# The last third of a feed-forward down projection: six plain accumulations against seven block products

## The chip, the cores and the metric

The kernel runs on one core of a Trainium2 chip. The time is the device time of one execution in microseconds (us); lower is better. The engines are named as the profile names them: PE is the matrix engine, PEld its weight load, DVE the vector engine, ACT the scalar engine, POOL the general engine that also issues DMAs, SP the engine that only issues DMAs.

## The reference, cut to what matters

The model is a two-layer decoder trunk on 512 tokens of width 1024 in float32. Each layer ends in a gated feed-forward block with 2816 hidden columns, and the change lies in its last matrix product, `@ w_down`.

```python
def swiglu(h, w_gate, w_up, w_down):
    return (jax.nn.silu(h @ w_gate) * (h @ w_up)) @ w_down
...
for i in range(DEPTH):                       # DEPTH = 2
    ...
    x = x + swiglu(rmsnorm(x, ffn_norm[i]), w_gate[i], w_up[i], w_down[i])
    if i == N_A_LAYERS - 1:                  # after layer 0
        kv = (rmsnorm(x, kv_norm) @ w_kv_shared)
return rmsnorm(x, final_norm)
```

After layer 0 the next work needs two normalised copies of `x` (for `b_in` and for `w_kv_shared`). After layer 1 only the final norm and the store of the output follow.

## The kernel before

**Three matmuls for one.** Every float32 operand is split into a high part (ACT copies it into a rounded type, `hi_of`, L153) and a low part (DVE subtracts, `lo_of`, L156). A product is three matmuls: high with high, high with low, low with high (`three`). Weights come by DMA into `raw` tiles (two buffers) and are split into `wh` and `wl` tiles (nine buffers with the tag "w", shared by high and low parts). The nine buffers let the splitting run about four weight pieces ahead of PE; a new piece waits until PE has done with an old one.

**The feed-forward block.** `ffn` (L797) takes the 2816 hidden columns in steps `c` of 256, eleven of them, in the groups of `FF_GROUPS`: steps 0 to 3, 4 to 7 and 8 to 10. In a step it makes gate and up (tiles `g` and `u`) for two tiles of 128 hidden columns, with all 512 tokens, and their product `sg`. After each group the group's part of the down projection is added onto the residual, the four tiles `xt[0]` to `xt[3]` (128 tokens by 1024 columns each, printed as `x`).

**Two ways for the down projection.** The first two groups (`SEVEN`) are done by `seven_products` (L713): tokens, hidden columns and output columns are halved, and the 2 by 2 block product, eight block products as it stands, is made from seven products of sums of blocks (Strassen's scheme in Winograd's form). `seven_lhs` makes the sums on the side of the hidden values, once for each step: `e`, `o`, `d` (128x512) and `n` (128x256), each split in high and low. The sums on the side of the weights are made by DMAs that add onto a tile in place (`accum_op=ALU.add`, issued by POOL) and by DVE adds (`plus`). The third group is done plainly, by `by_token` (L393): for each half of the 1024 output columns, for each of the four token tiles, the products over six tiles of hidden columns are summed in one bank (`d`), and `residual` adds the bank to `x`.

**What follows the third group.** For each token tile, when its second half is in, ACT makes the sum of squares (`square_sum`), DVE the mean (`ms`), POOL the power -1/2 (`rstd`), and `then` is called. In layer 0 that is `both_norms` (L862): `Normed.add` scales the tile to `xn_hmix`, and once two tiles are there, generators (`turn`) transpose them on PE and split them into `hmix1` and `hkv`. PE goes on with `first.run` (tiles `pb`): four products of 24 matmuls of 256 columns for tokens 0 to 255, then the same for tokens 256 to 511. In layer 1 `gained` multiplies `x` by the final gain, `finish` scales by `rstd` and SP stores the result.

**Order.** Each engine runs its instructions in the order in which a scheduler wrote them; `keep` and `keep_in_program_order` hold chosen ones in the order of the code.

Of the kernel before, what the change touches and what calls it, by code (L numbers as in the profile page):

```python
# [16 lines left out]
P = 128  # L17
# [23 lines left out]

SEVEN = FF_GROUPS[:2]
# [64 lines left out]
def trunk(ctx: ExitStack, tc: tile.TileContext, x, mem, mix_norm, a_in, conv_w, b_in,  # L107
# [38 lines left out]
    ordered = [True]  # L146

# [8 lines left out]
    def lo_of(dst, src, hi):  # L156
        keep(nc.vector.tensor_tensor(dst, src, hi.bitcast(F32), ALU.subtract))  # L157
# [111 lines left out]
    def rstd_of(ss, name):  # L269
        m = small.tile([P, 1], F32, tag="ms", name=f"ms_{name}")  # L270
        keep(nc.vector.tensor_scalar(m, ss[:, 0:1], ss[:, 1:2], EPS, ALU.add, ALU.add))
# [101 lines left out]
    class Opening:  # L373
# [5 lines left out]

        def prepare(self):  # L380
            self.gets = self.first() + self.second()
            self.w = [get() for get in self.gets[:2]]
# [107 lines left out]
    def zero_rows(kl):  # L490

        for hh in range(2):
            nc.gpsimd.memset(kl[HD - hh * HD:P - hh * HD, hh, :].bitcast(F32), 0.0)
# [205 lines left out]
    def seven_lhs(even, odd, name):  # L699

        h0, h1 = slice(0, 256), slice(256, 512)
# [14 lines left out]
        def at(operand, hl, t):  # L716
            y, hf = home[operand]
            return y[:, hl, hf * 256 + t * P:hf * 256 + (t + 1) * P]
# [3 lines left out]
    def seven_products(w, g0, lhs, name):  # L722

        n = len(lhs)
        rows4 = w[2 * g0 * P:2 * (g0 + n) * P, :].rearrange("(c two p) n -> p c two n", two=2, p=P)

        def block(i, j):
            return rows4[:, :, i, j * 512:(j + 1) * 512]

        def load(raw, first, second=None):  # L730
            tc.keep_in_program_order(nc.sync.dma_start(raw, block(*first)))
            if second is not None:
                tc.keep_in_program_order(nc.gpsimd.dma_start(raw, block(*second), accum_op=ALU.add))
            return raw

        def product(make, operand, raw):
            banks = [make(f"{operand}_{name}{t}") for t in range(2)]
            for c in range(0, n, 2):
                wp = split(raw[:, c:c + 2, :], 2, 512)
                for j in range(2):  # L740
                    for t in range(2):
                        three(banks[t], lambda hl: lhs[c + j](operand, hl, t), lambda hl: wp[hl][:, j, :],
                              c + j == 0, c + j == n - 1)
                        lanes.pump()
            return banks

        def copies(banks):
            held = [t2([P, S], F32, f"v_{name}{t}") for t in range(2)]
# [4 lines left out]
        def plus(dst, raw):  # L753
            for c in range(0, n, 2):
                nc.vector.tensor_tensor(dst[:, c:c + 2, :], dst[:, c:c + 2, :], raw[:, c:c + 2, :], ALU.add)

        def onto(t, hf, v, op=ALU.add):
            part = xt[t][:, hf * 512:(hf + 1) * 512]
            nc.vector.tensor_tensor(part, part, v, op)

        shape = [P, n, 512]
# [3 lines left out]
        v = copies(product(acc, "A11", r1))  # L765
        for t in range(2):
            onto(t, 0, v[t])
        u = copies(product(acc, "N1", r2))
# [28 lines left out]
    def ffn(layer, h, chains, opening, then, half=lambda t, hf: None):  # L797
        ss = sums(f"ssf{layer}")
        pending = []
        for g0, g1 in FF_GROUPS:  # L800
            hid = {}
            seven = (g0, g1) in SEVEN
            for c in range(g0, g1):
# [5 lines left out]
                for i in range(2):  # L809
# [14 lines left out]
                    if not seven:  # L824
                        hid[f] = split_y(sg, f"hid{layer}{f}")
                    elif i == 0:
                        even = sg
                    else:
                        hid[c] = seven_lhs(even, sg, f"hid{layer}{c}")
            if seven:  # L830
                pending += seven_products(w_down[layer], g0, [hid[c] for c in range(g0, g1)], f"d{layer}{g0}")
                continue
            last = g1 == 11
            for hf in range(2):
                def done(t, b):
                    residual(t, hf, b, ss if last else None, f"f{layer}{g0}")
                    if last:
                        half(t, hf)
                    if last and hf == 1:
                        then(t, rstd_of(ss[t], f"f{layer}{t}"))  # L840
                by_token(w_down[layer], [[2 * c, 2 * c + 1] for c in range(g0, g1)], hf * 512, 512,
                         ylhs(lambda k: hid[k]), NT, f"d{layer}{g0}{hf}", done, tail=TAIL if last and hf else 1)
# [19 lines left out]
    def both_norms(t, r):  # L862
        nq.add(t, xt[t], r)
        if t == 1:
            first.prepare()

    first = Opening(lambda i: acc(f"pb{i}"), lambda: cols(b_in[0], MAIN), lambda: cols(b_in[0], 0))
    ffn(0, h, nh.chains, opening, both_norms)
# [6 lines left out]
    for kl in key_lo:  # L875
        zero_rows(kl)
# [134 lines left out]
    def gained(t, hf):  # L1011
        if hf == 0:
# [11 lines left out]
    ffn(1, h, nh.chains, opening, finish, gained)  # L1024
# [26 lines left out]
```

## Time and profile before

| | |
|---|---|
| three runs, us | 1144.94, 1145.65, 1145.78 (median 1145.65) |
| profiled execution, us | 1145.12 |
| its span, first to last instruction, us | 1143.4 |
| mean granted clock of PE | 0.998 of full speed |
| PE busy, share of the span | 99% |
| DVE, ACT, POOL busy | 61%, 46%, 7% |
| third group of layer 0, first matmul to last | 524.45 to 558.85 us |
| third group of layer 1, first matmul to last | 1103.96 to 1136.6 us |

A row of the timeline gives the start in us from the start of the span, the time in us, engine, line, operation, "output<-inputs", and in brackets how long the engine stood idle before it and what ended that. A line of the kernel can be that of a helper. Rows of the chain of waits are start, length and what; rows of the groups give busy time, mean ns of one and idle time before. Where instructions of one engine follow each other closely their spans overlap, so what one costs there is the distance between starts.

### The profile page before, as it was taken

The page shows a single profiled execution, that of the slowest core. Times are in us where ns is not written, and L with a number is a line of the kernel's source. Part 1 is how long each engine was busy: PE and PEld are TensorE (multiplying, and loading weights), DVE is VectorE, ACT ScalarE, POOL GpSimd, SP SyncE. Part 2 cuts the span into 40 slices and gives each one's busy share as a digit, 9 for nine tenths or more (in the row PEclk, how much of TensorE's full clock was granted, in tenths as well). Part 3 has the DMA queues.
Part 4 walks back from the last instruction along what each step waited for, and adds up shares of the span by engine and source line. Part 5 has one row for each costly group of instructions (what it writes and reads, how often), then busy time and mean ns, then how long its engine had stood idle before and what let it go on. Part 6 is the DMA issues. An engine that isn't in the chain of part 4 may idle for free.

```text
span 1143.4 us, 14862 instructions
## 1 busy us (share of the span) xinstructions
PE 1130.9 (99%) x5844; PEld 963.2 (84%) x5844; DVE 699.5 (61%) x1044; ACT 524.1 (46%) x896; POOL 76.3 (7%) x155
## 2 busy tenths in 40 slices
PE   9999999999999999999999999999999999999997
PEld 9898888988888888888988988788888888888886
DVE  5767453553774468434678799986546844485335
ACT  7555423533432344233666677665434332353223
POOL 1100000000000001000100123321000000000000
PEclk9999999999999999999999999999999999999999
DMA  8332422247332742414222211122274244542311
GB/s 259 111 111 74 144 78 74 74 142 190 111 111 74 219 108 79 141 62 130 75 74 75 74 56 56 38 75 92 74 220 123 66 143 149 109 148 76 126 57 74
DMA packets 97456, 122.10 MB, mean 107 GB/s; under 512 B 2217, under 2 KB 73963, under 8 KB 97387
## 3 DMA queue, kind: packets, MB, share of 16 engines
q1 hardware_dynamic: 93040, 112.73, 30.1%
q0 software_dynamic: 4224, 8.39, 4.3%
q8 instruction: 46, 0.75, 0.3%
q14 instruction: 23, 0.19, 0.1%
q10 hardware_dynamic: 123, 0.03, 0.0%
HBM read 119.05 MB, written 2.10 MB: 106 GB/s over the span
## 4 chain that ended last, share of the span: by engine, by line
PE 92%; issue 3%; DVE 2%; ACT 1%; POOL 1%; DMA 1%; POOLq 0%; ACTq 0%; SPq 0%; DVEq 0%
PE u L136 22%; PE g L136 19%; PE A_d L136 6%; PE d L136 5%; PE o L136 5%; PE N_d L136 4%; PE S_d L136 4%; PE gu L136 4%; PE bg L136 3%; PE v L136 3%; PE k L136 2%; PE pa L136 2%; PE cg L136 2%; PE q L136 1%; PE pb L136 1%
## 5 line engine op out<-in xcount | busy, mean ns | idle before, releaser
L157 DVE TENSOR_TENSOR wl<-raw,wh 128x1024 fp32r<-128x1024 f32 x180 | 220.0, 1222 | 281.3 <-PE u L136 136.5
L154 ACT ACTIVATE wh<-raw 128x1024 fp32r<-128x1024 f32 x180 | 191.0, 1061 | 264.6 <-PE u L136 75.8
L819 ACT ACTIVATE sg<-g 128x512 f32<-128x512 f32 x40 | 23.9, 598 | 105.5 <-PE g L136 105.5
L136 PE MATMUL g<-hffn0h,wh 128*128 128x512 f32 x160 | 62.3, 389 | 0.0
L136 PE MATMUL g<-hffn0l,wh 128*128 128x512 f32 x160 | 62.3, 389 | 0.0
L136 PE MATMUL g<-hffn1h,wh 128*128 128x512 f32 x160 | 62.3, 389 | 0.0
L136 PE MATMUL g<-hffn1l,wh 128*128 128x512 f32 x160 | 62.3, 389 | 0.0
L136 PE MATMUL g<-hffn0h,wl 128*128 128x512 f32 x160 | 62.2, 389 | 0.0
L136 PE MATMUL u<-hffn0h,wh 128*128 128x512 f32 x160 | 62.2, 389 | 0.0
L136 PE MATMUL u<-hffn0l,wh 128*128 128x512 f32 x160 | 62.2, 389 | 0.0
L136 PE MATMUL u<-hffn0h,wl 128*128 128x512 f32 x160 | 62.2, 389 | 0.0
L136 PE MATMUL g<-hffn1h,wl 128*128 128x512 f32 x160 | 62.2, 389 | 0.0
L136 PE MATMUL u<-hffn1h,wh 128*128 128x512 f32 x160 | 62.2, 389 | 0.0
L136 PE MATMUL u<-hffn1l,wh 128*128 128x512 f32 x160 | 62.2, 389 | 0.0
L136 PE MATMUL u<-hffn1h,wl 128*128 128x512 f32 x160 | 62.2, 389 | 0.0
L136 PE MATMUL d<-wh,hid 128*128 128x512 f32 x192 | 59.7, 389 | 0.0
L154 ACT ACTIVATE wh<-b_d 128x1024 fp32r<-128x1024 f32 x32 | 33.7, 1060 | 34.2 <-PE u L136 15.3
L920 DVE TENSOR_TENSOR_SCAN sn<-sn 128x127 f32<-128x127 f32 (+3 forms) x48 | 40.3, 840 | 4.8 <-POOL sn L901 4.4
L136 PEld LDWEIGHTS d<-wh,hid 128*128 128x128 f32 x192 | 36.0, 188 | 7.5
L157 DVE TENSOR_TENSOR wl<-b_d,wh 128x1024 fp32r<-128x1024 f32 x32 | 38.9, 1221 | 4.1 <-PE N_d L136 2.3
L136 PE MATMUL d<-wl,hid 128*128 128x512 f32 x96 | 37.4, 389 | 0.0
L136 PEld LDWEIGHTS u<-hffn0l,wh 128*128 128x128 f32 x160 | 30.0, 188 | 6.3
(777 smaller groups left out, 2937.9 us busy)
## 6 DMA issues: line engine op xcount, KB each, us to landing
raw<-in_w_gate_dram SPq DMA_DIRECT2D x22, 1024.0 KB, 5.3
raw<-in_w_up_dram SPq DMA_DIRECT2D x22, 1024.0 KB, 5.4
raw<-in_w_down_dram SPq DMA_DIRECT2D x12, 1024.0 KB, 6.6
raw<-in_a_in_dram SPq DMA_DIRECT2D x8, 1024.0 KB, 5.5
b_d<-in_w_down_dram SPq DMA_DIRECT2D x8, 1024.0 KB, 7.5
raw<-in_w_o_dram SPq DMA_DIRECT2D x12, 512.0 KB, 3.6
raw<-in_w_kv_shared_dram SPq DMA_DIRECT2D x6, 1024.0 KB, 5.0
raw<-in_w_mem_kv_dram SPq DMA_DIRECT2D x4, 1024.0 KB, 5.2
```

Of the source, the lines that this page charges most:

```text
L136: nc.tensor.matmul(dst, a, b, start=start, stop=stop)
L154: keep(nc.scalar.activation(dst, src, AF.Copy))
L157: keep(nc.vector.tensor_tensor(dst, src, hi.bitcast(F32), ALU.subtract))
L819: nc.scalar.activation(sg, bg, AF.Silu)
L920: nc.vector.tensor_tensor_scan(back, back, back, 1.0, ALU.mult, ALU.bypass)
```

## The change

The third group of each layer is made by seven block products too, in a function of its own, `last_products`. Their order is S3, S2, A11, N1, A22, A12, N4. The halves of the tokens are exchanged in `seven_lhs` for that group, so that tokens 0 to 255 are complete after the fifth product (A22) and tokens 256 to 511 after the seventh (N4). The weight sums T3 and T2 are loaded ahead by one SP load each with one and two accumulating DMAs; T1 and T4 are then made in the same tiles in two pieces (`change`), T1 by SP loads with accumulating POOL DMAs behind them, T4 by accumulating POOL DMAs; the block B22 is loaded into T1's tile. Ten times in a layer, a result that goes into a second place of `x` is added there by a POOL DMA from a copy (`dma_onto`). The loads and splits of the next stage's first weights (`first` in layer 0) are called at fixed places within the group, and `zero_rows` (memsets of `kl`) is held in program order behind it.

```diff
-SEVEN = FF_GROUPS[:2]
...
-    def seven_lhs(even, odd, name):
-
-        h0, h1 = slice(0, 256), slice(256, 512)
+    def seven_lhs(even, odd, last, name):
+
+        h0, h1 = (slice(256 * (i ^ last), 256 * (i ^ last) + 256) for i in range(2))
...
+    def dma_onto(t, hf, v):
+        tc.keep_in_program_order(nc.gpsimd.dma_start(x_part(t, hf), v, accum_op=ALU.add))
...
+    def last_products(w, g0, lhs, name, ss, half, then, opening):
...
+        r2 = load(big_tile(shape, F32, f"t3_{name}"), (0, 1), (1, 1))
+        r1 = load(big_tile(shape, F32, f"t2_{name}"), (0, 0), (0, 1), (1, 1))
+        r3 = load(raw_tile(shape), (0, 0))
+        r4 = load(raw_tile(shape), (1, 0))
+        b3 = product(att, "S3", s.pieces(r2))
+        s.change(r2, (0, 0), (0, 1), anew=True)
+        b2 = product(acc, "S2", s.pieces(r1))
+        s.change(r1, (1, 0))
+        p, _ = parts(r3)
+        if opening is not None:
+            opening.load()
+        v = s.copies(b2, "v")
+        d = [t2([P, S], F32, f"d_{name}{t}") for t in range(2)]
+        for t in range(2):
+            dma_onto(2 + t, 1, v[t])
+            nc.vector.tensor_tensor(d[t], b3[t], v[t], ALU.subtract)
+            onto(t, 1, d[t], ALU.subtract)
+        b1 = product(acc, "A11", p)
+        p, _ = parts(r2)
+        s.change(r2, (1, 1), anew=True)
+        for t in range(2):
+            onto(t, 0, b1[t])
+            onto(t, 1, b1[t], ALU.subtract)
+            dma_onto(t, 0, d[t])
+            both = slot([P, 2, S], F32, f"a11_{name}{t}")
+            for i, sign in enumerate((1.0, -1.0)):
+                nc.scalar.activation(both[:, i, :], b1[t], AF.Copy, scale=sign)
+                dma_onto(2 + t, i, both[:, i, :])
+        bu = product(acc, "N1", p)
+        p, _ = parts(r1)
+        u = s.copies(bu, "u")
+        for t in range(2):
+            onto(t, 1, bu[t])
+            squares(t, 1)
+            half(t, 1)
+            dma_onto(2 + t, 1, u[t])
...
+        p12, before = parts(r4)
+        product(att, "A22", p, c21)
+        if opening is not None:
+            opening.load()
+            opening.split()
+        for t in range(2):
+            then(t, rstd_of(ss[t], f"{name}{t}"))
+        p, before = parts(r2)
+        if opening is not None:
+            opening.split()
+        for t, b in enumerate(product(att, "A12", p12)):
+            with tc.issue_after(before.ins):
+                onto(2 + t, 0, b)
+            squares(2 + t, 0)
+            half(2 + t, 0)
...
+        def c12(t, b):
+            with tc.issue_after(last_ms[0].ins):
+                onto(2 + t, 1, b)
+            squares(2 + t, 1)
+            half(2 + t, 1)
+            then(2 + t, rstd_of(ss[2 + t], f"{name}{2 + t}"))
+
+        product(acc, "N4", p, c12)
...
-                    if not seven:
-                        hid[f] = split_y(sg, f"hid{layer}{f}")
...
-            last = g1 == 11
-            for hf in range(2):
-                def done(t, b):
-                    residual(t, hf, b, ss if last else None, f"f{layer}{g0}")
...
+            if not last:
+                pending += seven_products(w_down[layer], g0, lhs, f"d{layer}{g0}")
+            else:
+                last_products(w_down[layer], g0, lhs, f"d{layer}{g0}", ss, half, then, opens)
```

Three places show how the instructions move. The first is the end of DVE's order, in layer 1. Before, each add of a finished bank onto the residual (`x<-d,x`; x_75 and x_76 are token tiles 2 and 3) has one gain product (`out`), one mean and one scaling behind it, and no weight split stands among them:

```order
L645 TENSOR_TENSOR x_75<-d_9670,x_75 128x512
L1015 TENSOR_TENSOR out_9655<-x_75,g_final 128x512
L271 TENSOR_SCALAR ms_f_9770<-ss_ssf_7314 128x1
L1019 TENSOR_SCALAR out_9655<-out_9655,rstd_f_9772 128x512
L645 TENSOR_TENSOR x_76<-d_9671,x_76 128x512
L1015 TENSOR_TENSOR out_9666<-x_76,g_final 128x512
L271 TENSOR_SCALAR ms_f_9800<-ss_ssf_7315 128x1
L1019 TENSOR_SCALAR out_9666<-out_9666,rstd_f_9802 128x512
```

In the changed kernel the same end of DVE's order reads as follows (`A_d` is the bank of A12, `N_d` that of N4, `wl` the low part of N4's second weight piece):

```order
L156 TENSOR_TENSOR wl_9933<-t_d_9693,wh_9932 128x1024
L813 TENSOR_TENSOR x_75<-x_75,A_d_9936 128x512
L813 TENSOR_TENSOR x_76<-x_76,A_d_9937 128x512
L1150 TENSOR_TENSOR out_9959<-x_75,g_final 128x512
L1150 TENSOR_TENSOR out_9964<-x_76,g_final 128x512
L813 TENSOR_TENSOR x_75<-x_75,N_d_9966 128x512
L1150 TENSOR_TENSOR out_9959<-x_75,g_final 128x512
L271 TENSOR_SCALAR ms_d_9980<-ss_ssf_7415 128x1
L813 TENSOR_TENSOR x_76<-x_76,N_d_9988 128x512
L1154 TENSOR_SCALAR out_9959<-out_9959,rstd_d_9982 128x512
L1150 TENSOR_TENSOR out_9964<-x_76,g_final 128x512
L271 TENSOR_SCALAR ms_d_10002<-ss_ssf_7416 128x1
```

Both halves of tiles 2 and 3 now come together at the end, with the last weight split ahead of them, and the add of the last bank stands behind tile 2's mean.

The second place is POOL's order in layer 0, from the T4 pieces (`t_d_4287`) to the first power of the third group (`rstd`); before, no DMA stood in this stretch, and the four powers followed the memsets of `kl`:

```order
L764 DMA t_d_4287<-in_w_down_dram 128x2x512
L764 DMA t_d_4287<-in_w_down_dram 128x512
L816 DMA x_75<-v_d_4367 128x512
L816 DMA x_76<-v_d_4368 128x512
L816 DMA x_73<-d_d_4371 128x512
L816 DMA x_75<-a_d_4412 128x512 x2
L816 DMA x_74<-d_d_4372 128x512
L816 DMA x_76<-a_d_4420 128x512 x2
L816 DMA x_75<-u_d_4453 128x512
L816 DMA x_76<-u_d_4454 128x512
L274 TENSOR_TENSOR rstd_d_4507<-ms_d_4505,minus_half 128x1
```

All ten DMAs onto `x` (x_73 is token tile 0) now stand ahead of tile 0's power.

The third place is DVE's order at the end of the third group of layer 0. Before, the add of the last bank onto tile 3 (x_76) has hkv splits around it and a weight split of `b_in` (`wl`) behind it:

```order
L323 SCALAR_TENSOR_TENSOR hkvl_2001<-tr_hmix_4467,p_cols,hkvh_1997 128x256
L645 TENSOR_TENSOR x_76<-d_4355,x_76 128x512
L323 SCALAR_TENSOR_TENSOR hkvl_2001<-tr_hmix_4467,p_cols,hkvh_1997 128x256
L323 SCALAR_TENSOR_TENSOR hkvl_2002<-tr_hmix_4476,p_cols,hkvh_1998 128x256
L271 TENSOR_SCALAR ms_f_4541<-ss_ssf_2007 128x1
L157 TENSOR_TENSOR wl_4690<-raw_4430,wh_4689 128x1024
```

In the changed kernel that add stands behind the last of the hkv splits, and two weight splits of `b_in` stand between it and tile 3's mean:

```order
L324 SCALAR_TENSOR_TENSOR hkvl_2002<-tr_hmix_4569,p_cols,hkvh_1998 128x256
L301 TENSOR_SCALAR xn_hmix_4626<-x_75,rstd_d_4624 128x512
L324 SCALAR_TENSOR_TENSOR hkvl_2003<-tr_hmix_4578,p_cols,hkvh_1999 128x256
L813 TENSOR_TENSOR x_76<-x_76,N_d_4629 128x512
L156 TENSOR_TENSOR wl_4750<-raw_4499,wh_4749 128x1024
L156 TENSOR_TENSOR wl_4791<-raw_4499,wh_4790 128x1024
L271 TENSOR_SCALAR ms_d_4642<-ss_ssf_2007 128x1
L301 TENSOR_SCALAR xn_hmix_4646<-x_76,rstd_d_4644 128x512
```

So tile 3 is normalised later in DVE's order than before, by the hkv splits and one weight split.

## Rows read from the trace of the kernel before

**Rows 1.** The page: busy us, share of the span, instructions.

```profile
PE 1130.9 (99%) x5844; PEld 963.2 (84%) x5844; DVE 699.5 (61%) x1044; ACT 524.1 (46%) x896; POOL 76.3 (7%) x155
```

**Rows 2.** The chain that ended last: start, us, what.

```profile
524.45 28.56 PE d L136 x126
553.01 1.75 PE tr_hmix L143 x16
554.76 4.09 PE d L136 x18
558.85 5.39 PE pb L136 x45
...
1103.96 28.57 PE d L136 x126
```

**Rows 3.** Stretches: us, busy time of each engine, clock, DMA share, GB/s.

```profile
524.50:558.80 34.30, 34.30 (x161) 28.65 (x160) 16.69 (x27) 15.90 (x31) 1.66 (x3) 1.00 0.20 63
558.80:570.00 11.20, 11.20 (x97) 11.20 (x96) 9.96 (x22) 9.65 (x24) 1.46 (x1) 1.00 0.55 185
```

**Rows 4.** Timeline of DVE, the end of layer 1.

```profile
1136.63 0.69 DVE L645 TENSOR_TENSOR x<-d,x 128x512 f32<-128x512 f32 x1 [1.17 <-PE d L136]
1137.36 0.69 DVE L1015 TENSOR_TENSOR out<-x,g_final 128x512 f32<-128x512 f32 x1
```

**Rows 5.** Timeline of ACT, the end of layer 1.

```profile
1137.42 0.63 ACT L267 ACTIVATE junk_f<-x 128x512 bf16<-128x512 f32 x1 [1.72 <-DVE x L645]
...
1139.05 0.72 ACT L1020 ACTIVATE out<-out,rstd_f 128x512 f32<-128x512 f32 x1 [0.91 <-POOL rstd_f L273]
```

**Rows 6.** Timeline of DVE, seven products of the second group, layer 0.

```profile
457.23 1.22 DVE L157 TENSOR_TENSOR wl<-raw,wh 128x1024 fp32r<-128x1024 f32 x1
458.36 0.69 DVE L759 TENSOR_TENSOR x<-x,v_d 128x512 f32<-128x512 f32 x1
458.96 1.28 DVE L759 TENSOR_TENSOR x<-x,A_d 128x512 f32<-128x512 f32 x2
```

**Rows 7.** Groups of DVE by form, 413 to 460 us: busy, mean ns.

```profile
L157 DVE TENSOR_TENSOR hid07o<-sg,hid07o 128x512 fp32r<-128x512 f32 x1 | 0.7, 686 | 0.0
L702 DVE TENSOR_TENSOR ns_hid<-sg,sg 128x256 f32<-128x256 f32 x1 | 0.4, 427 | 0.0
```

**Rows 8.** Timeline of DVE, weight splits ahead of the third group, layer 0.

```profile
507.94 1.22 DVE L157 TENSOR_TENSOR wl<-raw,wh 128x1024 fp32r<-128x1024 f32 x1 [2.15 <-PE g L136]
...
524.31 1.23 DVE L157 TENSOR_TENSOR wl<-raw,wh 128x1024 fp32r<-128x1024 f32 x1 [4.27 <-PE u L136]
```

**Rows 9.** DMA issues by line: KB each, median us from issue to landing.

```profile
t_d<-in_w_down_dram POOLq DMA_DIRECT2D x4, 1024.0 KB, 8.8
...
raw<-in_w_down_dram SPq DMA_DIRECT2D x4, 512.0 KB, 3.6
out_dram<-out SPq DMA_DIRECT2D x8, 256.0 KB, 2.3
```

**Rows 10.** Timeline of POOL, second and third group, layer 0.

```profile
389.81 1.28 POOL L733 DMA_DIRECT2D t_d<-in_w_down_dram  x1 [110.94 <-DVE wl L157]
...
550.80 0.55 POOL L273 TENSOR_TENSOR rstd_f<-ms_f,minus_half 128x1 f32<-128x1 f32 x1 [3.44 <-DVE ms_f L271]
```

**Rows 11.** DMA rate in 40 slices of 384 to 415 us (0.78 us each).

```profile
GB/s 386 388 386 388 388 280 3 0 0 0 108 116 190 203 206 209 211 275 412 381 352 53 21 0 0 42 151 114 201 206 201 211 196 32 0 0 0 0 0 0
```

**Rows 12.** Timeline of ACT, splits of the transposed tiles, layer 0.

```profile
553.86 0.62 ACT L267 ACTIVATE junk_f<-x 128x512 bf16<-128x512 f32 x1
554.38 0.19 ACT L267 ACTIVATION_READ_ACCUMULATOR junk_f<-x 128x1 f32 x1
554.47 1.56 ACT L321 ACTIVATE hmix1h<-tr_hmix,m_cols 128x256 fp32r<-128x256 f32 x4
```

**Rows 13.** Timeline of DVE behind the third group of layer 0.

```profile
561.63 0.68 DVE L645 TENSOR_TENSOR x<-d,x 128x512 f32<-128x512 f32 x1
...
563.29 1.22 DVE L157 TENSOR_TENSOR wl<-raw,wh 128x1024 fp32r<-128x1024 f32 x1
...
565.21 0.48 DVE L300 TENSOR_SCALAR xn_hmix<-x,rstd_f 128x512 f32<-128x512 f32 x1
```

More of the change, by code (lines that the diff above doesn't have):

```diff
@@ L146, in trunk @@
     ordered = [True]
+    last_lo, last_ms = [None], [None]
     def keep(ins):
@@ L378, in __init__, with load, split @@
             self.first, self.second = first, second
+            self.gets, self.w = [], []
+        def load(self):
+            self.gets += self.second() if self.gets else self.first()
+        def split(self):
+            self.w.append(self.gets[len(self.w)]())
         def prepare(self):
-            self.gets = self.first() + self.second()
-            self.w = [get() for get in self.gets[:2]]
+            for step in (self.load, self.load, self.split, self.split):
+                step()
         def run(self, feat, chains, order=lambda i: None):
@@ L751, in copies, with plus, x_part, onto @@
             return held
[L753 to L761, printed above, removed]
+    def plus(dst, raw):
+        for c in range(0, dst.shape[1], 2):
+            nc.vector.tensor_tensor(dst[:, c:c + 2, :], dst[:, c:c + 2, :], raw[:, c:c + 2, :], ALU.add)
+    def x_part(t, hf):
+        return xt[t][:, hf * 512:(hf + 1) * 512]
+    def onto(t, hf, v, op=ALU.add):
+        return nc.vector.tensor_tensor(x_part(t, hf), x_part(t, hf), v, op)
+    def dma_onto(t, hf, v):
+        tc.keep_in_program_order(nc.gpsimd.dma_start(x_part(t, hf), v, accum_op=ALU.add))
+    def seven_products(w, g0, lhs, name):
+        s = Blocks(w, g0, lhs, name)
+        load, shape = s.load, s.shape
+        def product(make, operand, raw, by_tile=None):
+            return s.product(make, operand, s.pieces(raw), by_tile)
         r1 = load(big_tile(shape, F32, f"b11_{name}"), (0, 0))
@@ L798, in ffn @@
+    def ffn(layer, h, chains, opening, then, opens=None, half=lambda t, hf: None):
         ss = sums(f"ssf{layer}")
@@ L801, in ffn @@
             hid = {}
-            seven = (g0, g1) in SEVEN
+            last = g1 == FF_GROUPS[-1][1]
             for c in range(g0, g1):
@@ L823, in ffn @@
                     del pending[:3]
-                    if not seven:
-                        hid[f] = split_y(sg, f"hid{layer}{f}")
-                    elif i == 0:
+                    if i == 0:
                         even = sg
                     else:
[L829 to L832, printed above, removed]
-            last = g1 == 11
-            for hf in range(2):
-                def done(t, b):
-                    residual(t, hf, b, ss if last else None, f"f{layer}{g0}")
[L837 to L842, printed above, removed]
+                        hid[c] = seven_lhs(even, sg, last, f"hid{layer}{c}")
+            lhs = [hid[c] for c in range(g0, g1)]
+            if not last:
+                pending += seven_products(w_down[layer], g0, lhs, f"d{layer}{g0}")
+            else:
+                last_products(w_down[layer], g0, lhs, f"d{layer}{g0}", ss, half, then, opens)
     def ys(k):
@@ L1011, in gained @@
     def gained(t, hf):
-        if hf == 0:
+        if t not in xg:
             xg[t] = slot([P, D], F32, f"out{t}")
```

107 lines of the change are left out of this document (74 added, 33 removed).

## The prediction, made before the changed kernel ran

> **What bounds the kernel now.** I read the page first: PE is busy for 99% of the span, DVE for 61% [rows 1]. Then the chain that ended last, at the third group of both layers: it is PE alone, 144 matmuls in layer 0 (126 and 18, with 16 transposes between them) and as many in layer 1 [rows 2]. 28.56 us for 126 is 0.2267 us a matmul, 1.75 for 16 transposes 0.11 each, and 5.39 for the 45 matmuls of 256 columns behind them 0.12 each. Then the stretches: PE is busy for 34.30 of 34.30 us in the third group of layer 0 and for 11.20 of 11.20 us behind it, while DVE is busy for 16.69 and 9.96 [rows 3]. So every matmul taken away is time gained, as long as nothing else becomes late. What follows is therefore a count of PE's gain, and then of what DVE, ACT and POOL owe at the two ends of the group.
>
> **What is removed on PE.** Six tiles of hidden columns by two halves by four token tiles by three matmuls are 144; seven products by three steps by two token tiles by three are 126. 18 fewer are 4.08 us a layer, 8.16 us in all [rows 2]. Nothing else of PE is changed.
>
> **What is added elsewhere.** I count time t from the end of the last gate and up matmul, 524.45 in layer 0 and 1103.96 in layer 1. Where DVE runs without a gap, a low part of 128x1024 costs 1.13 us (start to start), one of 128x512 or an add onto `x` 0.60 to 0.64 [rows 6]; a 256 wide one 0.34, a scaling of 512 columns 0.40 (estimates, by the same shift, from 0.43 and 0.48) [rows 7, 13].
>
> *DVE in layer 1*, from t = 0 to the add of the last bank, by the order: the second piece of S2 (0.60), the product `sg` and the sums and low parts of step 10 (3.9), five products' low parts at 1.13 and 0.60 (8.65), two differences d (1.2), thirteen adds onto `x` (8.3), seven gain products (4.5), three means and two scalings (1.4). That is 28.5 us against PE's 28.57: DVE, which had half its time free, has none left. I laid the rows one behind the other and let each wait for its inputs: weight buffers hold it up at t = 6.2 for 0.4, the ACT copies of N1 at 16.9 for 0.5, tile 2's square sum at 29.9 for 0.2, and each restart costs 0.1, about 1.8 in all. So the last add starts at t = 30.3, not at PE's end. Before it started at 1136.63, t = 32.67 [rows 4]. From that add to the end of ACT's last scaling are 3.14 us before [rows 4, 5]; now tile 2's scaling on ACT stands ahead of tile 3's square sum, some 0.6 more. Gain of layer 1: 32.67 + 3.14 - 30.3 - 3.75 = **1.8 us**, of 4.08.
>
> PE itself waits for nothing in that group by the same laying out. The tightest places: the hidden step 10 (`d`, high part at t = 3.24, low at 4.2; PE wants them at 3.4 and 4.3, since the order puts three matmuls of S2 ahead), and the low part of N4's pieces (24.7 and 26.1, wanted at 24.7 and 26.1).
>
> *The weight sums* I cost at nothing. Splits run ahead: the third group's first low part was made 16.5 us before its first matmul, the fourth at its start [rows 8]. So T3's first piece is free at t = -15.3, and T1 needs a load of 512 KB (3.6) and an accumulation (at most 8.8) [rows 9]: ready by t = -2.5, second piece by 2.5; DVE reaches them at 6.6 and 8. T4 starts when S2 is split (t = -4.4 and 0.5) and is there at 4.4 and 9.3, wanted at 11.0 and 14.8. That cover is 4 to 9 us; without it, each us late is one of PE's.
>
> *Layer 0, where the next stage starts.* Without waits PE would reach the second half of `pb` at t = 28.56 + 3.5 + 96 x 0.12 = 43.6, before 47.65. The waits, by the same laying out: the transposes of tile 1 for its scaling, behind a weight split of `b_in` and two of N4 on DVE (0.5); `pb`'s fourth bank (0.25); the third weight of `b_in` (1.0); tile 3's scaling (0.65). The last two come from one place. ACT has 16 splits of 0.39, three square sums of 0.72, a weight's high part and a scaling ahead [rows 12], 10.1 us from t = 26.2, and DVE's low parts follow each; the add of the last bank stands behind them, at 36.85, 6 us after N4 ends. Before, it came 2.8 us after the end of `d`, with one weight split behind it and the scaling at 565.21 [rows 13]. Now two weight splits stand behind it, and tile 3 is scaled at t = 41.2. Sum 2.4 us: gain 1.65 without POOL.
>
> *POOL* is the unknown. Before, it issued only accumulations of 1024 KB, 1.28 us of POOL each, landing after 8.8 [rows 9, 10]. Now ten of 256 KB stand ahead of tile 0's power. Let one cost POOL c and land L after its issue. The plus and minus copies of A11's first tile are ready at t = 14.2 (DVE must read the bank first); from the plus copy on POOL issues minus, d onto tile 1, two onto tile 3 and u, and the last u waits until the minus copy on the same half has landed. The power can start at 14.2 + 5c + L. It is wanted at 22.7 in layer 0, and by 24.0 in layer 1. For c the bounds are 0.55, a tiny POOL instruction, and 1.28 [rows 10]; I take 1.0, since the rows to describe are a quarter. For L they are 2.3, a plain store of 256 KB, and 8.8 [rows 9]. Of the 8.5 of one accumulation the data moved for some 5.3 us, at about 205 GB/s [rows 11]; a quarter of that and the fixed 3.1 are 4.4, and with the smaller c 4.1, which I take. So the power starts at 23.3: 0.6 late in layer 0, nothing in layer 1. Gain of layer 0: 1.65 - 0.6 = **1.05 us**.
>
> The Trainium skill, DMA: Bandwidth & Descriptors, Anatomy of one DMA (SWDGE path), fits such a DMA as 2.0 us plus bytes by 436 GB/s. That is 2.6 us for 256 KB, with which the 0.6 would vanish and the sum be 1142.2; for 1024 KB it gives 4.4 where the trace has 8.8, so I don't go by it. The same page, Rules for kernel authors, wants the earlier DMA's semaphore waited for before an accumulation onto the same bytes; that is the wait of the last u.
>
> **The sum.** 1.8 + 1.05 = 2.85 us. The profiled execution took 1145.12 us, 0.5 below the median of 1145.65; both would fall by that, the median to 1142.8. 0.2%, about what a measurement of this kernel can tell, is 2.3 us.
>
> **The rivals.**
>
> *All of PE's gain arrives* (1137.5 us). It would if DVE's restarts and ACT's order cost less than I laid out and the ends hide. For it: PE waits for nothing inside the group. Against: DVE's 28.5 us of work alone, and the last add behind 20 rows in layer 0.
>
> *POOL eats the gain* (about 1145.4). With c = 1.28 and L = 4.4 the power comes at 25.0, 2.3 late in layer 0 and about 1 in layer 1: gain 0.2. From 5c + L = 8.5 on each us costs one in layer 0, from about 9.8 in layer 1 too.
>
> *Slower: small accumulations land as late as large ones* (about 1155). The minus copy onto tile 2 goes onto the half that v went to at t = 8.35, and POOL waits for that landing with d for tile 1 queued behind. With L = 8.5 minus goes out at 16.9, d at 18.1 and lands at 26.6; DVE's add of A22 onto tile 1, wanted at 20.6, waits 6 us, and behind it in order stand N4's splits, so PE stops. Some 6 us a layer, 12 less the 2.85: 9 slower. It decides from L = 4.4 on; the gain is gone at 5.4, and 2.3 are lost at 6.7. For it: the only accumulations in the trace. Against: their size, and the store's 2.3.
>
> That 126 matmuls don't take the place of 144 is excluded by the order.
>
> **How the numbers follow.** Chances: my forecast (gain 1.5 to 5) 0.55, all of PE's gain or nearly 0.17, POOL eats it 0.20, slower 0.08. Most of the forecast lies above 2.3: 0.42 faster and 0.13 the same. Faster 0.42 + 0.17 = 0.59, same 0.13 + 0.20 = 0.33, slower 0.08. The range: half of the 0.17 lies below 1139.0; above 1145.6 lie the slower case and a little of POOL's. 1139.0 to 1145.6 leaves out 0.18.
>
> **What would show it.** PE without a gap from S3 to N4 in layer 1, 28.6 us, and the last add of DVE 1 to 2 us after PE's last matmul (before: at once). In layer 0 the first of `pb` about 31 us after the last gate and up matmul, then PE idle twice, before the low part of the third `b_in` weight and before tile 3's transposes. On POOL, ten DMAs of some 1.0 us, landing near 4, the first power within 1 us of its mean. I am wrong if the weight sums release a split in PE's idle time (T1 late), if the landings exceed 5 us, or if DVE is done before PE at the end.

## The result, and the profile after

The changed kernel took 1151.74 us (median of four runs, 1150.68 to 1153.43), the kernel before, in runs beside it, 1145.40 (1144.94 to 1145.78). The ratio is 1.0058 with an interval of 1.0046 to 1.007: slower by 6.3 us, where a gain of 2.85 was forecast. The profiled execution of the changed kernel took 1150.68 us, its span 1149.0. The line of the page that answers to [rows 1]:

```profile
PE 1128.1 (98%) x5808; PEld 956.9 (83%) x5808; DVE 733.1 (64%) x1112; ACT 545.4 (47%) x940; POOL 109.7 (10%) x189
```

The 36 matmuls are gone (5844 to 5808). To see where the time went, four starts divide each span: the first matmul of the third group in layer 0 (A), the first of the `q` product of the next stage (B), the first of the third group in layer 1 (C), and the end of the span (D).

| kernel, profiled run | A | B | C | D | A to B | C to D |
|---|---|---|---|---|---|---|
| before | 524.28 | 583.46 | 1103.80 | 1143.4 | 59.18 | 39.60 |
| changed | 524.95 | 589.01 | 1109.30 | 1149.0 | 64.06 | 39.70 |

Between B and C both take 520.3. So layer 0 lost 4.9 us from A to B, where PE's saving is 4.08; layer 1 neither lost nor won; and 0.7 was lost ahead of A, in groups that the prediction held to be unchanged.

In layer 0 PE ran from S3 to A12 without a wait of 0.1 us. Then came the first three of these rows, which are all of PE's idle time there; the last row is from layer 1, its one long wait (timeline of PE):

```profile
554.00 0.44 PE L141 MATMUL tr_hmix<-ident,xn_hmix 128*128 128x128 f32 x2 [4.16 <-DVE xn_hmix L301]
555.88 2.40 PE L141 MATMUL tr_hmix<-ident,xn_hmix 128*128 128x128 f32 x10 [0.97 <-DVE xn_hmix L301]
572.65 1.53 PE L141 MATMUL tr_hmix<-ident,xn_hmix 128*128 128x128 f32 x12 [0.18 <-DVE xn_hmix L301]
...
1137.71 0.50 PE L134 MATMUL N_d<-wl,hid110n 128*128 128x512 f32 x1 [1.46 <-DVE wl L156]
```

The transposes wait for the scaling of tile 0, and the chain of waits says what that waited for. Here it is from the end of S2 on, cut to the longer pieces (start, length, what):

```profile
532.88 0.60 ACT v_d L802
...
533.78 6.62 DMA x<-v_d
...
...
542.52 8.93 DMA x<-a_d
...
551.98 0.86 POOL x L816
552.84 0.60 POOL rstd_d L274
...
555.34 0.49 DVE xn_hmix L301
...
555.88 2.40 PE tr_hmix L141 x10
558.28 3.41 PE N_d L134 x8
```

Two landings, 6.62 and 8.93 us, stand where the prediction had 4.1. On POOL the first one cost little, since the copy that waited for it was itself ready only at 539.9 (POOL stood idle for 0.32 us ahead of it). POOL's own timeline shows the second one as a long wait:

```profile
541.98 2.43 POOL L816 DMA_DIRECT2D x<-a_d  x2
546.05 0.86 POOL L816 DMA_DIRECT2D x<-u_d  x1 [1.63 <-DMA x<-a_d]
551.98 0.86 POOL L816 DMA_DIRECT2D x<-u_d  x1 [5.07 <-DMA x<-a_d]
552.54 0.88 POOL L274 TENSOR_TENSOR rstd_d<-ms_d,minus_half 128x1 f32<-128x1 f32 x1
```

DVE's timeline adds that the mean of tile 0 (`ms_d`) had been ready since 548.9, while the power began at 552.54:

```profile
546.97 0.69 DVE L813 TENSOR_TENSOR x<-x,A_d 128x512 f32<-128x512 f32 x1 [2.11 <-DMA x<-d_d]
548.71 0.20 DVE L271 TENSOR_SCALAR ms_d<-ss_ssf 128x1 f32<-128x1 f32 x1
553.46 0.49 DVE L301 TENSOR_SCALAR xn_hmix<-x,rstd_d 128x512 f32<-128x512 f32 x1 [3.42 <-POOL rstd_d L274]
```

Why they land late is in the stretches of that time (columns as in [rows 3]; the last two are the mean busy share of the 16 DMA engines and what they moved):

```profile
533.00:537.00 4.00, 4.00 (x20) 3.30 (x19) 3.87 (x7) 2.66 (x4) 1.75 (x2) 1.00 1.07 359
537.00:541.00 4.00, 4.00 (x19) 3.34 (x18) 3.70 (x7) 2.16 (x4) 1.80 (x3) 1.00 1.08 221
541.00:545.00 4.00, 4.00 (x20) 3.30 (x19) 3.62 (x5) 4.00 (x10) 3.42 (x4) 1.00 1.13 203
545.00:549.00 4.00, 4.00 (x20) 3.30 (x18) 2.03 (x4) 2.79 (x6) 0.86 (x1) 1.00 1.11 180
549.00:553.00 4.00, 0.84 (x4) 0.38 (x2) 1.05 (x1) 0.00 (x0) 1.02 (x2) 1.00 1.04 280
```

The engines are full for 20 us on end. Until 537 they carry plain loads of SP alone (weights of `b_in`, B22), at 359 GB/s; then mostly accumulations at 180 to 221, near the rate that [rows 11] show for one large one; and from 549 on mostly plain loads again. Eight of the ten accumulations, 2.1 MB, were issued within 9 us, and at 205 GB/s they alone take 10; SP's loads of the stretch, 2.83 MB, take 8 more at 359. In front of the accumulations was no free engine but a queue, and not of their own kind alone. POOL's DMA queue (q0) and SP's (q1) from 531 to 553 (packets, MB, share of 16 engines), then the medians from issue to landing (columns as in [rows 9]):

```profile
q0 software_dynamic: 1188, 2.17, 58.6%
q1 hardware_dynamic: 2432, 2.83, 40.6%
x<-a_d POOLq DMA_DIRECT2D x4, 256.0 KB, 5.6
x<-v_d POOLq DMA_DIRECT2D x2, 256.0 KB, 6.9
x<-d_d POOLq DMA_DIRECT2D x2, 256.0 KB, 4.9
x<-u_d POOLq DMA_DIRECT2D x2, 256.0 KB, 7.4
```

In layer 1, where no weights of a next stage are loaded, the last copy of A11 still took 7.45 us (the chain, and a stretch of that time):

```profile
1126.57 7.45 DMA x<-a_d
...
1127.00:1131.00 4.00, 4.00 (x19) 3.31 (x18) 3.42 (x6) 3.36 (x8) 2.27 (x3) 1.00 1.10 183
```

So the accumulations make a queue by themselves; what the loads of `b_in` add to it in layer 0 was not tried apart.

A second loss follows the first. Behind the long wait PE's granted clock fell to 0.50, and was back at 1.00 by 562:

```profile
553.00:557.00 4.00, 2.02 (x9) 1.59 (x10) 2.88 (x6) 2.98 (x5) 0.97 (x2) 0.72 0.67 127
557.00:565.00 8.00, 8.00 (x36) 6.76 (x36) 5.84 (x14) 6.72 (x19) 0.55 (x1) 0.71 0.43 131
...
555.00:561.00 6.00, 5.12 (x17) 4.51 (x18) 4.42 (x8) 5.36 (x12) 0.00 (x0) 0.50 0.47 129
562.00:565.00 3.00, 3.00 (x20) 2.64 (x19) 2.72 (x8) 2.81 (x9) 0.55 (x1) 1.00 0.02 6
```

A mean of 0.71 is a mixture of the full 2.4 GHz and of 1.2 GHz: the eight matmuls of N4 in the chain above took 3.41 us, 0.43 each, instead of 0.2267 [rows 2]. PE's 10 busy us from 553 to 565, at 0.71 to 0.72, held 2.9 us less work. So from A to B: 5.3 us idle and 2.9 by the clock, less the 4.08 saved, are 4.1 of the 4.9; the other 0.8 is what is left over, delays too short to stand as waits.

### The profile page after: what moved, and what is told of

It is laid out like the page before. It is cut to its first block, busy times and chain, and to the rows that moved or that the text cites. A ratio compares the mean times of both kernels' runs of the same rounds, so it can differ in the third digit from the quotient of the medians.

```text
span 1149.0 us, 15039 instructions
## 1 busy us (share of the span) xinstructions
PE 1128.1 (98%) x5808; PEld 956.9 (83%) x5808; DVE 733.1 (64%) x1112; ACT 545.4 (47%) x940; POOL 109.7 (10%) x189
## 4 chain that ended last, share of the span: by engine, by line
PE 87%; issue 4%; DMA 3%; DVE 2%; POOL 2%; ACT 1%; POOLq 0%; DVEq 0%; ACTq 0%
PE u L134 22%; PE g L134 19%; PE A_d L134 6%; PE o L134 5%; PE S_d L134 5%; PE N_d L134 4%; PE gu L134 4%; PE v L134 3%; PE bg L134 3%; PE pa L134 2%; PE q L134 2%; PE cg L134 2%; PE k L134 2%; DMA x<-a_d 1%; PE pb L134 1%
## 5 line engine op out<-in xcount | busy, mean ns | idle before, releaser
L156 DVE TENSOR_TENSOR wl<-raw,wh 128x1024 fp32r<-128x1024 f32 x176 | 212.5, 1209 | 249.7 <-PE u L134 119.2
L153 ACT ACTIVATE wh<-raw 128x1024 fp32r<-128x1024 f32 x176 | 184.8, 1050 | 234.9 <-PE u L134 80.2
L752 POOL DMA_DIRECT2D t_d<-in_w_down_dram x10 | 13.0, 1298 | 531.6 <-DMA t_d<-in_w_down_dram 305.7
L156 DVE TENSOR_TENSOR wl<-t_d,wh 128x1024 fp32r<-128x1024 f32 (+1 forms) x28 | 28.9, 1031 | 43.9 <-PE u L134 31.4
L153 ACT ACTIVATE wh<-t_d 128x1024 fp32r<-128x1024 f32 (+1 forms) x28 | 25.4, 907 | 38.6 <-issue 25.9
L134 PEld LDWEIGHTS u<-hffn1h,wh 128*128 128x128 f32 x160 | 30.1, 188 | 6.3
```

The source lines that it names most:

```text
L134: nc.tensor.matmul(dst, a, b, start=start, stop=stop)
L153: keep(nc.scalar.activation(dst, src, AF.Copy))
L156: last_lo[0] = nc.vector.tensor_tensor(dst, src, hi.bitcast(F32), ALU.subtract)
L752: tc.keep_in_program_order(nc.gpsimd.dma_start(raw, self.block(*of), accum_op=ALU.add))
```

## The experiments

**Theory A**: the accumulations onto `x` queue on the same DMA engines, so the last copy of A11 lands late, POOL waits for it ahead of the last `u`, and tile 0's power stands behind that in POOL's order. **Theory B**: the order of DVE and ACT around the last products stalls PE, whatever POOL does. **Theory C**: what costs is POOL's own time to issue ten DMAs. **Theory D**: the clock fell because PE stood still, and that costs some 3 us by itself. All times are medians; the profiled runs:

| run | A | B | C | D | A to B | C to D | median us | ratio to before, interval |
|---|---|---|---|---|---|---|---|---|
| e1_powers_first | 524.87 | 584.80 | 1105.04 | 1144.7 | 59.93 | 39.66 | 1147.29 | 1.0021, 1.0011 to 1.003 |
| e2_fold_u | 524.77 | 583.62 | 1103.78 | 1142.5 | 58.85 | 38.72 | 1144.00 | 0.9989, 0.998 to 0.9998 |
| e3_no_dma | 524.95 | 583.19 | 1103.68 | 1141.4 | 58.24 | 37.72 | 1143.08 | 0.998, 0.9971 to 0.9989 |
| e4_fill_pe | 524.93 | 588.29 | 1110.17 | 1150.3 | 63.36 | 40.13 | 1151.91 | 1.0058, 1.0041 to 1.0075 |
| e5_only_u | 525.29 | 583.51 | 1103.91 | 1141.6 | 58.22 | 37.69 | 1143.34 | one run |
| e6_fold_delay | 525.43 | 588.73 | 1109.21 | 1148.0 | 63.30 | 38.79 | 1149.47 | 1.003, 1.0019 to 1.0041 |
| e7_fold_order | 524.72 | 583.19 | 1103.39 | 1142.1 | 58.47 | 38.71 | 1143.84 | 0.9984, 0.9976 to 0.9993 |
| e8_fold_d_dve | 524.95 | 581.35 | 1101.12 | 1140.5 | 56.40 | 39.38 | 1142.22 | 0.9969, 0.9957 to 0.9981 |
| e9_d_dve_layer0 | 524.56 | 580.98 | 1100.96 | 1139.7 | 56.42 | 38.74 | 1141.42 | 0.9963, 0.9949 to 0.9977 |
| e10_old_order | 524.66 | 589.66 | 1109.82 | 1149.5 | 65.00 | 39.68 | 1150.83 | 1.0042, 1.0029 to 1.0055 |

**e1, the powers ahead of the last accumulations.**

```diff
             half(t, 1)
-            dma_onto(2 + t, 1, u[t])
...
             then(t, rstd_of(ss[t], f"{name}{t}"))
+        for t in range(2):
+            dma_onto(2 + t, 1, u[t])
```

> Only the place of the two accumulations of u on POOL's queue is changed: they stand behind the powers of tiles 0 and 1 instead of ahead of them. Theory A (the power of tile 0 is held by POOL's wait for the landing of the last copy of A11, since the accumulations share the same DMA engines and land 6 to 9 us after their issue): its mean was ready at 548.9 and the power started at 552.5, so the power comes some 3.5 us earlier, PE's idle time behind A12 in layer 0 falls from 5.3 to about 1.5 us, the low clock behind it (3.7 us) goes for the most part, and the kernel takes 1143.5 to 1146.5 us. In layer 1 the two scalings come 1.8 us earlier, but the last accumulation is no earlier, so at most 1 us there. Theory B (the loss is in DVE's and ACT's order around the last three products, whoever releases the power): the stall only moves to another row, 1149 us or more. Theory C (POOL's own time to issue ten DMAs, 0.9 to 1.2 us each): only the two DMAs of u leave, 1.7 us, and 1149 to 1150.

POOL's timeline of this run in layer 0:

```profile
549.47 1.47 POOL L274 TENSOR_TENSOR rstd_d<-ms_d,minus_half 128x1 f32<-128x1 f32 x1 [4.48 <-DVE ms_d L271]
...
552.17 0.88 POOL L816 DMA_DIRECT2D x<-u_d  x1
```

And PE's, the first wait behind A12:

```profile
551.51 0.44 PE L141 MATMUL tr_hmix<-ident,xn_hmix 128*128 128x128 f32 x2 [1.72 <-DVE xn_hmix L301]
```

The power now waits for its mean, not for a DMA, and starts 3.1 us earlier; PE's wait ahead of the transposes is 1.72 instead of 4.16, and the clock stayed at 1.00. 4.45 us came back, nearly all of it in layer 0 (A to B 64.06 to 59.93). That is more than the 1.7 us of issue time that C allows and goes against B. The time misses the expected range by 0.8: the power took 1.47 us where 0.55 was reckoned, PE's idle time summed to 3.6, and layer 1 won nothing, as its last `u` now goes out later.

**e2, eight accumulations.**

```diff
+        u = []
...
-            both = slot([P, 2, S], F32, f"a11_{name}{t}")
-            for i, sign in enumerate((1.0, -1.0)):
-                nc.scalar.activation(both[:, i, :], b1[t], AF.Copy, scale=sign)
-                dma_onto(2 + t, i, both[:, i, :])
+            a11 = t2([P, S], F32, f"a11_{name}{t}")
+            nc.scalar.activation(a11, b1[t], AF.Copy)
+            dma_onto(2 + t, 0, a11)
+            u.append(a11)
...
-        u = s.copies(bu, "u")
         for t in range(2):
             onto(t, 1, bu[t])
+            w = t2([P, S], F32, f"u_{name}{t}")
+            nc.vector.tensor_tensor(w, bu[t], u[t], ALU.subtract)
+            u[t] = w
```

> The difference of N1 and A11 is made by DVE from the bank and one SBUF copy, and goes onto tiles 2 and 3 as one accumulation instead of two: eight accumulations instead of ten, four ACT copies of 0.6 us fewer, two DVE differences of 0.6 us more in each layer. Theory A: no accumulation waits for another's landing any more except u for v, 0.5 MB of 2.5 fewer stand in the queues, POOL reaches the power of tile 0 with its mean (548.5), PE's idle time falls to about 1.5 us, and the time is 1143 to 1146 us. Theory B: DVE has 1.2 us more in each layer and nothing is won, 1151 to 1154. Theory C: two DMAs of POOL less, 1149.5.

POOL's timeline, from the first `u` on:

```profile
542.48 0.86 POOL L816 DMA_DIRECT2D x<-u_d  x1 [0.26 <-DMA x<-v_d]
543.68 0.86 POOL L816 DMA_DIRECT2D x<-u_d  x1 [0.34 <-DVE u_d L910]
548.39 1.47 POOL L274 TENSOR_TENSOR rstd_d<-ms_d,minus_half 128x1 f32<-128x1 f32 x1 [3.85 <-DVE ms_d L271]
```

POOL is through with the DMAs 8 us earlier and idle when the mean arrives; PE's waits are 0.73, 0.51 and 0.26. 7.7 us came back by the medians, 5.2 of them from A to B and 1.0 from C to D in the profiled runs, although DVE does 1.2 us more in each layer: as A expected, and this version is already a little faster than the kernel before.

**e3, no accumulation onto `x`.**

```diff
     def dma_onto(t, hf, v):
-        tc.keep_in_program_order(nc.gpsimd.dma_start(x_part(t, hf), v, accum_op=ALU.add))
+        pass
```

> The ten accumulations onto x of the third group are left out in both layers (so v, d, u and A11 are missing from half of x), all else stays. Theory A: nothing holds the power but its mean; PE waits 0 to 1.5 us in layer 0, at full clock, and layer 1 gives its 1.8 us: 1140 to 1143.5 us. Theory B: the same order of DVE and ACT stalls PE as before: 1148 us or more. Between the two lies the case that the extra instructions cost part of it, 1144 to 1147.

The time is as A expected. The run also measures the terms of the prediction that have nothing to do with POOL: C to D falls from 39.60 to 37.72, 1.9 us, and A to B from 59.18 to 58.24, 0.9 us; PE's waits in layer 0 are these (its timeline):

```profile
551.79 1.31 PE L141 MATMUL tr_hmix<-ident,xn_hmix 128*128 128x128 f32 x10 [0.97 <-DVE xn_hmix L301]
564.08 0.39 PE L134 MATMUL pb<-hmix1h,wl 128*128 128x256 f32 x1 [0.18 <-DVE wl L156]
566.84 1.53 PE L141 MATMUL tr_hmix<-ident,xn_hmix 128*128 128x128 f32 x12 [0.71 <-DVE xn_hmix L301]
```

**e4, PE kept busy in the stall.** With all ten accumulations, work is added:

```diff
+        if opening is not None:
+            spare = acc(f"fill_{name}")
+            for i in range(18):
+                nc.tensor.matmul(spare, lhs[0]("A22", HI, i % 2), p12[0][1][HI][:, 0, :], start=True, stop=True)
         for t, b in enumerate(product(att, "A12", p12)):
```

> 18 more matmuls (4.1 us at full clock) into a spare bank stand ahead of A12 in layer 0, so that PE works while the power of tile 0 is late; nothing waits for them. Theory D (the clock fell because PE stood still, and the slower matmuls behind the stall cost 3.7 us by themselves): PE's idle time falls to 0.1 to 1.3 us, the granted clock stays at 1.00 to the end of the stage, N4's matmuls take 0.23 us again, and the time is 1147.5 to 1149 although the power comes no earlier. Against it: if the low clock has another cause (the DMA traffic, the activity of the other engines), or if the stall is all of the loss, the time stays at 1151 to 1152.5.

The stretches that answer to the two slow ones of the changed kernel:

```profile
553.00:557.00 4.00, 1.73 (x10) 1.04 (x9) 1.62 (x5) 2.25 (x4) 2.00 (x3) 1.00 0.73 146
557.00:565.00 8.00, 7.28 (x44) 5.97 (x43) 7.41 (x16) 7.38 (x18) 0.55 (x1) 1.00 0.39 132
```

The clock stayed at 1.00, with waits of 1.33 us at most, though the power came 1.3 us later than in the changed kernel. The time did not fall; 1151.91 is what was expected if the stall is all of the loss. But more than the filling had changed: the last copy of A11 landed 1.3 us later than in the changed kernel, the scheduler put the transposes in another order, and 1.6 us were lost between B and C. From the end of tile 0's power to B it took 33.6 us (554.68 to 588.29), in the changed kernel 35.6 (553.42 to 589.01). So the first half of D holds (with PE's waits at 1.33 us or less, the clock did not fall), and the price in the total is not measured by this run.

**e5, two accumulations alone.** Only `u` is kept (`v`, `d` and A11 are missing from half of `x`).

```diff
-    def dma_onto(t, hf, v):
+    def dma_onto(t, hf, v, go=False):
+        if not go:
+            return
...
-            dma_onto(2 + t, 1, u[t])
+            dma_onto(2 + t, 1, u[t], True)
```

> Only the two accumulations of u onto tiles 2 and 3 are kept of the ten in each layer (v, d and A11 are missing from half of x). Theory A says that one accumulation of 256 KB by itself lands in about 4.1 to 4.6 us, as the prediction took it, and that the 6 to 9 us of the changed kernel are the queue of ten on the same engines: the two land 4.0 to 5.0 us after their issue in both layers, the DMA engines are busy for less than 6 us of it. The other reading, that the size was estimated wrongly and a single one takes as long: 6 us or more here too. The time should be that of the kernel without accumulations, 1142.5 to 1144.

Issue to landing in layer 1:

```profile
x<-u_d POOLq DMA_DIRECT2D x2, 256.0 KB, 3.9
```

The two are 3.3 and 4.4 us, as the prediction had estimated for one. In layer 0, where a 1 MB load of `b_in` starts before the second has landed, they took 3.9 and 6.1. So the size of one alone was right, and the queue was left out.

**e6, the stall made by hand.** The version of e2, with a late power and nothing else:

```diff
-        nc.gpsimd.tensor_tensor(r, m, minus_half, ALU.pow)
+        for i in range(times):
+            nc.gpsimd.tensor_tensor(r, m, minus_half, ALU.pow)
...
-            then(t, rstd_of(ss[t], f"{name}{t}"))
+            then(t, rstd_of(ss[t], f"{name}{t}", 9 if opening is not None and t == 0 else 1))
```

> The version with eight accumulations (1144.0 us) in which the power of tile 0 in layer 0 is made nine times over on POOL, so that its end comes 8 x 0.55 = 4.4 us later (or up to 0.88 each, 7) while DMA, DVE and ACT have the same work as there. Theory D (a long enough idle time of PE by itself brings the clock down, and the slower matmuls cost some 3 us on top of it): PE's first idle time grows from 0.7 to about 5 us, the granted clock of the 10 us behind it is 0.7 to 0.85, and the time is 1144.0 + 4.4 + 3 = 1151 to 1152. Against it (the clock falls for another reason, such as the accumulations): the clock stays at 1.00 and the time is 1148.4.

The stretches around the stall:

```profile
553.00:555.00 2.00, 0.00 (x0) 0.00 (x0) 0.00 (x0) 0.00 (x0) 1.76 (x4) 0.64 0.09 30
...
554.00:560.00 6.00, 4.11 (x15) 3.62 (x16) 4.21 (x8) 4.35 (x8) 2.08 (x4) 0.50 0.00 1
...
561.00:563.00 2.00, 2.00 (x12) 1.70 (x11) 1.35 (x3) 0.99 (x4) 0.00 (x0) 1.00 1.04 358
```

PE stood still for 5.53 us and its clock went to 0.50, with the DMA engines empty: no load on them is needed for it. But the price of 3 us that D named is not confirmed. The end of the power moved from 549.86 (e2) to 555.32; counted from A, which is itself 0.7 later in this run, that is 4.8 us. From A to B the stage grew by 4.45, less than that, although PE's 4.11 busy us at 0.50 held some 2 us less work. So nothing is left for the slow matmuls: PE's waits sum to 5.53 us against 1.50 in e2, and smaller delays of e2 went under the stall. In the total, 1149.47 lies between the two readings, 1151 and 1148.4.

**e7 and e10, the order of the matmuls.** `product` now does both steps of a weight piece for one token tile and then for the other; before, both tiles of one step. Taken back, on e2 (e7) and on the changed kernel itself (e10):

```diff
             for c, wp in pieces:
-                for t in range(2):
-                    piece(c, wp, t)
+                for j in range(min(2, n - c)):
+                    for t in range(2):
+                        three(banks[t], lambda hl: self.lhs[c + j](operand, hl, t), lambda hl: wp[hl][:, j, :],
+                              c + j == 0, c + j == n - 1)
+                        lanes.pump()
```

> The version with eight accumulations, and in all products of two banks the order of the matmuls within a weight piece as in the kernel before (both token tiles of one step, then the next step) instead of both steps of one token tile. In the changed kernel A11 of groups 1 and 2 of layer 0 took 0.2 to 0.3 us longer, and its first matmul of the last hidden step came 0.33 instead of 0.23 us after the one ahead: it is asked for 0.68 us earlier than before. If that is the 0.6 us by which the third group starts later in layer 0, the time is 1143.2 to 1143.6, against 1144.0. If not, 1143.9 to 1144.3.

> The changed kernel with all ten accumulations, and only the order of the matmuls within a weight piece taken back to that of the kernel before. In the traces A11 of groups 1 and 2 took 5.45 us with the old order and 5.68 to 5.70 with the new one, in both layers, and the group's first four products 21.76 to 21.97 us against 22.02 to 22.29: together 1.1 us in four groups. If nothing behind them gives that back, 1150.4 to 1150.9 instead of 1151.7. If the late power in layer 0 comes at the same place whenever the group begins, the time stays at 1151.2 to 1152.

In the changed kernel, group 1 of layer 0, A11's first matmul of the last hidden step starts 0.33 us behind its forerunner, and 0.23 is the pitch where nothing waits (timeline of PE):

```profile
298.61 0.39 PE L134 MATMUL A_d<-wh,hid02e 128*128 128x512 f32 x1
298.94 0.50 PE L134 MATMUL A_d<-wh,hid03e 128*128 128x512 f32 x1
```

With the old order A11 takes 5.44 to 5.46 us again, in both kernels, instead of 5.67 to 5.70, and from A11 to A12 it is 21.9 instead of 22.2 to 22.3 (groups 1 and 2 of layer 0, starts in the traces). As times, 0.9 us was won in e10, as expected, and 0.2 in e7, less than expected; both intervals overlap with those of the run they are to be compared with. In layer 1 the same stretch of a group takes 0.2 to 0.3 us longer with the new order, which does not show from B to C. So 0.3 us a group is shown in the traces of layer 0, and what it is worth at the end lies between 0.2 and 0.9.

**e8 and e9, a version that beats both.** On e7, `d` goes onto tiles 0 and 1 by DVE, in e9 in layer 0 only. The edit is shown as it stands in e9; e8 has `onto` alone.

```diff
-            dma_onto(t, 0, d[t])
+            (dma_onto if opening is None else onto)(t, 0, d[t])
```

> As the run with the old matmul order and eight accumulations, but d goes onto the lower half of tiles 0 and 1 by DVE (two adds of 0.6 us) instead of POOL's accumulations: six are left, and tile 0's sum of squares no longer waits for a landing. If the landing is what holds tile 0's mean (0.6 us in layer 0 with eight), 0.3 to 0.6 us faster than the run without it. If DVE is the limit (full in layer 1), 0.5 to 1.5 us slower.

> As the run with six accumulations, but d goes onto tiles 0 and 1 by DVE in layer 0 only; layer 1, where DVE has no time left, keeps POOL's accumulation of d. From the first matmul of the third group to the next stage layer 0 took 56.4 us with DVE and 58.5 with POOL, and layer 1 to the end of the span 39.4 with DVE and 38.7 with POOL. If these two add up as they stand, 0.7 us is won: 1141.4 to 1141.8 us, against 1142.2. If the rows of layer 1 differ by chance, 1142.0 to 1142.5.

e8 won 1.6 us on e7, more than either reading: 2.1 from A to B, less 0.7 from C to D, where DVE has no time to give. From A to B more changed than the landing of `d`: the scheduler put four matmuls of N4 ahead of the first transposes, where e7 has none, and PE's wait ahead of those transposes is gone (timelines of PE, first e7, then e8):

```profile
550.06 0.44 PE L141 MATMUL tr_hmix<-ident,xn_hmix 128*128 128x128 f32 x2 [0.42 <-DVE xn_hmix L301]
...
549.69 0.62 PE L134 MATMUL N_d<-wh,hid08n 128*128 128x512 f32 x2
...
550.60 0.42 PE L141 MATMUL tr_hmix<-ident,xn_hmix 128*128 128x128 f32 x2
```

PE's waits from A to B sum to 1.18 us in e7 and 0.51 in e8; most of the rest came out of short delays among the `pb` matmuls. So these runs do not part the landing from the order, and what the landing alone is worth is not settled. In e9 both came out as added up, 1141.42 us: 0.37% faster than the kernel before, 10.3 us faster than the changed one. One wait of PE is left in layer 0 ahead of B (its timeline in e9):

```profile
552.09 1.31 PE L141 MATMUL tr_hmix<-ident,xn_hmix 128*128 128x128 f32 x10 [0.51 <-DVE xn_hmix L301]
```

With six accumulations in layer 0 the copies of A11 land in 3.5 us instead of 5.6 (issue to landing, from 525 to 575):

```profile
x<-a_d POOLq DMA_DIRECT2D x2, 256.0 KB, 3.5
```

## Why the prediction was wrong

**What held.** PE's saving of 4.08 us a layer; no wait from S3 to A12, so the weight sums were in time, as costed at nothing; DVE as the limit of layer 1 (its gain of 1.8 is 1.9 in e3, where DVE is busy for 27.95 of 30 us from 1104 on). In layer 0 the gain without POOL was forecast at 1.65, and e3 has 0.9; PE's waits there sum to 1.9 us against the 2.4 laid out, but 1.3 more went in delays too small to stand as waits, which were not counted.

**The step that failed is L**, the landing of an accumulation: "a quarter of that and the fixed 3.1 are 4.4, and with the smaller c 4.1, which I take". It priced each of the ten as if it were alone. e5 shows that this is right for one alone (3.3 to 4.4), and the stretches that ten in a row, with SP's loads among them, are a queue: 16 engines full, some 200 GB/s, 8.93 us for the one that POOL waited for. The prediction had named the sign itself: "if the landings exceed 5 us". The rest of the POOL step was sound: 14.2 + 5c + L with the measured c of 0.86 and L of 8.93 is 27.4, and the power started at 552.54, 27.4 us after the end of the last gate and up matmul at 525.11. That it fits to 0.1 us is luck: the first copy went out 0.4 us later than 14.2, and POOL's issues followed each other at 0.5 to 1.2 us, not at one c. The want of 22.7 was right too (the power starts at 22.8 in e3); in the changed kernel even the mean was there only at 23.8, because the add that waited 2.11 us for `d` stands ahead of it in DVE's order. The Trainium skill, DMA: Bandwidth & Descriptors, Rules for kernel authors, says that DMAs of different issuing engines run on the same 16 engines and interleave; this trace agrees, with SP's loads and POOL's accumulations together at 1.04 to 1.13 of the engines from 533 to 553. That sentence speaks against each sum of landings that is made one by one.

**The rival that came true was given 0.08.** "Small accumulations land as late as large ones" had the mechanism and a price of about 1155. Its place was another: the add of A22 onto tile 1 waited 2.11 us for `d` in layer 0, not 6, and no split of N4 behind it held PE there. In layer 1 one did, for 1.46 us, but that split stood behind the two scalings that waited for the power. The price came from the power, which the rival did not follow. Against it stood "their size, and the store's 2.3": a store is no accumulation, and the size counts only once the bytes of all are added up. The first eight, 2.1 MB issued within 9 us, at the 205 GB/s of [rows 11], could have been worked out from what the prediction had shown.

**What was costed at nothing and was not**: the matmul order ("Nothing else of PE is changed"), 0.3 us in a group of layer 0 by the traces; and the clock behind a long wait of PE, which the prediction nowhere considered. Its price stays open: 2.9 us by the stretches of the changed kernel, some 2 by the comparison with e4, nothing in e6. Of the 0.7 us lost ahead of A, taking the order back (e10) returned 0.3, by one profiled run each; the other 0.4 is not explained.

**In layer 1** the forecast had POOL hide within its limit ("nothing in layer 1"). There the last `u` waited too, for 3.47 us, the two powers came at 1135.11, 25.7 us after the end of the last gate and up matmul (1109.46) against the 24.0 allowed, and DVE, PE and the end followed. The 1.8 us went there.

## What to carry to other kernels

Before pricing DMAs one by one, add up the bytes of all that are in flight in the stretch, at the rate of their kind, and lay them on one set of engines; an instruction that needs nothing of them must not stand behind their issue on the same queue. Accumulating the same place twice makes the second DMA wait for the first to land: one DVE operation that makes the sum first was cheaper here than the landing. A stall of the matrix engine behind which its clock falls may cost more than its length: some 2.9 us more by the stretches of the changed kernel, nothing more in e6.

## What the runs showed of the hardware that was not expected

An accumulating DMA keeps the DMA engines busy for nearly twice as long as a plain load of the same bytes: 180 to 203 GB/s (541 to 549, almost only accumulations) against 359 (533 to 537, plain loads alone), at the same full busy share. The size of the packets is not the reason: over the trace of the changed kernel a packet of 2 KB took 194 ns on POOL's queue and 93 on SP's (means).

The granted clock of PE stayed at 1.00 behind waits of 1.72 us (e1) and 1.84 (e10, layer 1), and fell to 0.50 where the wait was 4.16 (changed, 0.50 from 555 to 561), 5.53 (e6, from 554 to 560) and 6.49 us (e10, from 554 to 560). In e6 and e10 it fell while PE still stood; in the changed kernel just after PE had begun again, so that more work lay under the low clock there.

The power of tile 0, 128 by 1 elements, took 0.55 us of POOL in the kernel before ([rows 10]) and 1.47 in e1 and e2, where a low part of 1.2 us started on DVE right behind the mean. Whether one causes the other was not tried.
